# Ten moving tiles of the gate/up matmuls, moved to other SBUF offsets

## The chip, the cores and the metric

The kernel runs on one NeuronCore of a Trainium2 chip. The metric is device microseconds for one execution. The kernel before takes 2365.82 us (median of 2 runs, 2365.75 to 2365.89).

## What is computed

The reference is a two-layer encoder trunk over 1024 tokens of width 1024. Each layer has a combined input projection, three kinds of attention, an output projection, and a SwiGLU feed-forward part. All arrays are float32. The change is in the feed-forward part:

```python
h = rms_norm(x, g_ffn[l]) * (1 + sc_f) + sh_f
gate, up = split_cols(h @ w_gu[l], (FFN_HIDDEN, FFN_HIDDEN))
x = x + gt_f * ((jax.nn.silu(gate) * up) @ w_down[l])
```

`h` is 1024 tokens by 1024 features, `w_gu` is 1024 by 5632, and `FFN_HIDDEN` is 2816.

## The kernel before

Precision. Every float32 operand of a large matmul is split into a high part and a low part (type fp32r), and a product is three matmuls: high weights by high activations, low weights by high activations, high weights by low activations (`mm3`, line 202). The helper `split_to` makes such a pair: ScalarE writes the high part, VectorE or GpSimd the low part.

Gate/up as a fast matrix product. `h` and `w_gu` are cut into 2 by 2 blocks, and a Winograd-like scheme with seven products takes the place of eight (`PRODUCTS`, line 217). The activations are the moving operand, 512 tokens wide. They stand in seven pairs of tiles, made once per layer, each of shape 128 x 4 x 512 with 8192 bytes in a partition: `h21`, `h11`, and `ht2`, `ht1`, `ht4`, `h22`, `ht3`. A letter `h` or `l` at the end of the tile's name is the high or the low part. The helper that allocates them is `h_tiles` (line 2087): `h21` and `h11` come from a pool of their own (`ha`), the other five pairs from the pool `hb`. Both pools are on the right side of SBUF, which is a stack that grows towards lower addresses. The tiles of a pool lie one behind the other, with no space between.

The weights are the stationary operand. `a_parts` (line 233) makes the weight pieces `wpt` (128 x 2 x 4 x 128: high and low part of four blocks of 128 rows) in a ring of eight buffers of 4096 bytes.

The order of work. For each of 22 column groups (`NF`), and for each of the seven products, `product` (line 278) issues four `mm3`, that is twelve matmuls of 128 x 512, into one PSUM bank: `gu_product` (line 2199) then adds, copies or applies the activation. The first seven column groups do products 1 and 2 (`h11`, `h21`) ahead, with weights named `whi` and `wlo`, while `t2_part`, `t3_part` and `t4_part` make the other ten tiles. TensorE works the products in the order h11, h21, ht2, ht1, ht3, h22, ht4. Between the products of the later groups stand now and then two matmuls of another computation (`ps_mod`): their moving operands are `acch` and `accl`, and their weights are the constant tile `onesr`.

Behind gate/up comes the down projection (`ps_d`), whose weights and moving operand are both `wpt` tiles of the same ring. The raw weights of the down projection (`w11`, `w12`, `w21`, `w22`) are loaded by the SP queue into memory that the gate/up tiles held, and so some of these loads wait for TensorE's last reading of such a tile. The SP queue is issued in a fixed order.

Addresses in the built program. A start address within a partition, modulo 256, is called a tile's offset here. In the kernel before, the offset of all fourteen `h` tiles is 96, and so is that of every `wpt`, `whi` and `wlo` tile. `acch` and `accl` lie at 96 too, `onesr` at 128. A slice of an `h` tile starts at a multiple of 2048 bytes and a slice of the weights at a multiple of 512, so that the slices have their tile's offset.

Of the kernel before, what the change touches and what calls it, by code (L numbers as in the profile page):

```python
# [10 lines left out]
F32 = mybir.dt.float32  # L11
F32R = mybir.dt.float32r
# [7 lines left out]
P = 128  # L20
# [3 lines left out]
H = 512  # L24
# [61 lines left out]
def trunk(ctx: ExitStack, tc, A, C, out):  # L86
# [9 lines left out]
    def open_pool(name, bufs=1, side="left", space=None):  # L96
        kw = dict(name=name, bufs=bufs, side=side, reuse_waits="tile")
        if space is not None:
            kw["space"] = space
            if space == PSUM:  # L100
                kw.pop("side")
        cm = tc.tile_pool(**kw)
        p = cm.__enter__()
        return cm, p
# [432 lines left out]
    hl = hp.tile([P, KC, S], F32R, name="hl")  # L537
# [480 lines left out]
    for l in range(2):  # L1018
# [731 lines left out]
        class PairA(Band):  # L1750


            name, by_columns = "sA", True
# [11 lines left out]
        class PairB(Band):  # L1765
            name = "sB"
# [113 lines left out]
        for n in range(-AHEAD - 1, N + 3):  # L1880
# [74 lines left out]
            if n == 60:  # L1955
                t2 = [psS.tile([P, 2, H], F32, name="ps_o", tag="S") for _ in range(2)]
# [127 lines left out]
        ha_cm, hap = open_pool("ha", side="right")  # L2084
        hb = {}

        def h_tiles(pl, names):
            for b in names:
                hb[b] = [pl.tile([P, 4, H], F32R, name=f"h{b}{p}") for p in "hl"]

        h_tiles(hap, ("21", "11"))

        def h_norm(k, half, rows):
# [66 lines left out]

        ff_cm, ffp = open_pool("ffn", side="left")
        hb_cm, hbp = open_pool("hb", side="right")
        h_tiles(hbp, ("t2", "t1", "t4", "22", "t3"))
        turn = [-10]

        def x_tile(n, shape, name):
# [370 lines left out]
        for u in range(NU):  # L2537
# [14 lines left out]
            a, b = ahead.have.pop(0)  # L2552
# [18 lines left out]
            if num == 4:  # L2571
# [6 lines left out]
                else:  # L2578
                    h_cm, hp = open_pool("h", side="right")
                    hh = hp.tile([P, KC, S], F32R, name="hh")  # L2580
                    hl = hp.tile([P, KC, S], F32R, name="hl")
# [121 lines left out]
```

## Time and profile before

| | |
|---|---|
| median of the runs | 2365.82 us |
| span of the profiled execution, first to last instruction | 2365.0 us |
| TensorE busy | 2324.0 us (98%), 11804 matmuls |
| TensorE weight loads busy | 1959.2 us (83%) |
| VectorE / ScalarE / GpSimd busy | 1758.8 / 1185.8 / 778.4 us |
| mean granted TensorE clock | 0.998 |
| gate/up of layer 0, first to last of its matmuls | 552.6 to 981.3 us |
| gate/up of layer 1 | 1709.7 to 2134.9 us |

The profiled execution's own time was not kept beside its span; the span lies 0.8 us below the median of the runs.

How to read it: the matmuls overlap one another, so that a matmul's duration in the profile (389 ns for most with 512 columns) is a latency and not what it costs. What it costs in a stream is the distance from its start to the next matmul's start. The timeline view gives these starts in hundredths of a microsecond; where a row stands for several matmuls (x2), it gives the first one's start.

### The profile page before, as it was taken

Reading aid. Unit: us, or ns where it says so; the run is one execution under the profiler, and the core shown is the slowest. Engines: PE = TensorE matmul, PEld = TensorE weight load, DVE = VectorE, ACT = ScalarE, POOL = GpSimd, SP = SyncE. Lnnn points to the kernel's source line nnn. Section 1 sums busy time; section 2 is a strip of 40 time slices with the busy share of each in tenths; the row PEclk is TensorE's granted clock in tenths of the full one; section 3 lists DMA queues with packets and bytes.
Section 4 is the critical chain, followed back from the end, with each engine's and each line's share of the span. In section 5 each row is a group of like instructions: output and inputs, shape, how many; then the busy total and the mean of one; then the engine's idle time right before and its main releaser. Section 6 shows DMA issues by size and latency. Waiting matters only on the chain. (4 is left out here: it accounts for less than half of the span.)

```text
span 2365.0 us, 33492 instructions
## 1 busy us (share of the span) xinstructions
PE 2324.0 (98%) x11804; PEld 1959.2 (83%) x11804; DVE 1758.8 (74%) x2762; ACT 1185.8 (50%) x2262; POOL 778.4 (33%) x749
## 2 busy tenths in 40 slices
PE   9999999999999999999999999999999999999998
PEld 7888898888788888788888889988878888888886
DVE  7878998869867677595767689897796674538765
ACT  5423889845543333344633268896453434334443
POOL 1530447600444445100145134584005444430001
PEclk9999999999999999999999999999999999999999
DMA  8677416162435544775435851333634443339643
GB/s 281 182 213 232 116 34 185 51 210 94 146 121 166 165 138 141 232 233 181 148 102 139 249 177 28 92 104 104 208 98 139 151 147 103 99 107 305 203 120 112
DMA packets 307450, 358.02 MB, mean 151 GB/s; under 512 B 52029, under 2 KB 223901, under 8 KB 307281
## 3 DMA queue, kind: packets, MB, share of 16 engines
q1 hardware_dynamic: 290784, 346.26, 47.1%
q10 hardware_dynamic: 16128, 9.44, 1.5%
q8 instruction: 93, 1.52, 0.3%
q14 instruction: 77, 0.62, 0.1%
q0 software_dynamic: 368, 0.17, 0.0%
HBM read 270.84 MB, written 88.63 MB: 152 GB/s over the span
## 5 line engine op out<-in xcount | busy, mean ns | idle before, releaser
L49 PE MATMUL ps_d<-wpt 128*128 128x512 f32 x1848 | 423.7, 390 | 1.0 <-ACT wpt L49 0.7
L49 PEld LDWEIGHTS ps_d<-wpt 128*128 128x128 f32 x1848 | 345.7, 188 | 74.3 <-issue 3.0
L49 POOL TENSOR_SCALAR pr<-pr,rs 128x1024 f32<-128x1024 f32 (+2 forms) x248 | 190.7, 785 | 186.8 <-DVE rs L49 166.7
L49 POOL TENSOR_TENSOR sg<-sg,u 128x512 f32<-128x512 f32 x82 | 117.2, 1431 | 348.1 <-ACT sg L49 221.6
L49 ACT CAST wpt<-w 128x512 fp32r<-128x512 f32 x154 | 95.7, 621 | 194.5 <-PE ps_d L49 176.1
L49 PE MATMUL pv<-pt,vs 128*128 128x256 f32 x1088 | 174.0, 296 | 14.3 <-DVE y L49 13.0
L49 DVE TENSOR_TENSOR pt<-T,pt 128x512 fp32r<-128x512 f32 x272 | 177.4, 679 | 7.1 <-ACT pt L49 5.9
L49 ACT CAST pt<-T 128x512 fp32r<-128x512 f32 x272 | 151.7, 586 | 42.9 <-PE T L49 41.4
L49 DVE SCALAR_TENSOR_TENSOR acc<-wmt,condT,acc 128x512 f32<-128x512 f32 (+1 forms) x98 | 115.5, 1186 | 77.1 <-DMA wmt<-in_w_mod_dram 76.3
L49 POOL TENSOR_TENSOR wpt<-ws,wpt 128x512 fp32r<-128x512 f32 x80 | 112.8, 1410 | 181.6 <-ACT wpt L49 136.3
L49 ACT COPY u<-ps_w 128x512 f32<-128x512 f32 x128 | 75.1, 587 | 192.6 <-PE ps_w L49 192.6
L49 DVE TENSOR_TENSOR wpt<-w,wpt 128x512 fp32r<-128x512 f32 x154 | 109.0, 708 | 83.8 <-ACT wpt L49 83.8
L49 PEld LDWEIGHTS pv<-pt,vs 128*128 128x128 f32 x1088 | 141.0, 189 | 26.9 <-DVE y L49 24.9
L49 PE MATMUL T<-identr,pr 128*128 128x128 f32 x1176 | 160.1, 273 | 0.8 <-DVE pt L49 0.4
L49 PEld LDWEIGHTS T<-identr,pr 128*128 128x128 f32 x1176 | 137.8, 140 | 15.8 <-issue 1.3
L49 ACT CAST wpt<-ws 128x512 fp32r<-128x512 f32 x176 | 107.7, 622 | 53.3 <-PE ps_w L49 23.4
L49 DVE TENSOR_TENSOR wpt<-graw,wpt 128x512 fp32r<-128x512 f32 x154 | 110.2, 716 | 17.0 <-ACT wpt L49 17.0
L49 DVE TENSOR_TENSOR wpt<-ws,wpt 128x512 fp32r<-128x512 f32 x96 | 85.2, 896 | 47.6 <-ACT wpt L49 47.4
L49 DVE TENSOR_REDUCE rs<-sC 128x1 f32<-128x1024 f32 x88 | 107.4, 1220 | 12.3 <-PE sC L49 10.9
L49 DVE TENSOR_TENSOR ws<-wr 128x512 f32<-128x512 f32 x88 | 80.3, 913 | 48.5 <-POOL wpt L49 45.1
L49 ACT CAST wpt<-graw 128x512 fp32r<-128x512 f32 x154 | 95.0, 617 | 35.2 <-DMA graw<-gpd 31.0
L49 PE MATMUL ps_w<-h22h,wpt 128*128 128x512 f32 x352 | 108.9, 391 | 2.9 <-ACT u L49 1.9
(310 smaller groups left out, 5936.4 us busy)
## 6 DMA issues: line engine op xcount, KB each, us to landing
wr<-in_w_gu_dram SPq DMA_DIRECT2D x92, 512.0 KB, 4.2
gpd<-sg SPq DMA_DIRECT2D x154, 256.0 KB, 4.4
graw<-gpd SPq DMA_DIRECT2D x76, 512.0 KB, 3.8
w<-in_w_down_dram SPq DMA_DIRECT2D x110, 256.0 KB, 5.2
wmt<-in_w_mod_dram SPq DMA_DIRECT2D x48, 512.0 KB, 5.7
qk<-qkd SPq DMA_DIRECT2D x44, 512.0 KB, 7.3
wst<-in_w_o_dram SPq DMA_DIRECT2D x32, 512.0 KB, 4.3
wmt<-in_w_mod_dram SPq DMA_DIRECT2D x64, 256.0 KB, 4.0
```

Source lines behind the costliest of these rows:

```text
L49: ins = op(*args, **kwargs)
```

## The change

`h_tiles` gets an argument. With it, each tile is followed by a small tile of 8 floats (32 bytes) that nothing writes or reads. The five pairs of the pool `hb` are allocated with it, the two pairs of the pool `ha` without.

```diff
--- before.py
+++ after.py
@@ -2084,9 +2084,13 @@
         ha_cm, hap = open_pool("ha", side="right")
         hb = {}
 
-        def h_tiles(pl, names):
+        def h_tiles(pl, names, apart=0):
             for b in names:
-                hb[b] = [pl.tile([P, 4, H], F32R, name=f"h{b}{p}") for p in "hl"]
+                hb[b] = []
+                for p in "hl":
+                    hb[b].append(pl.tile([P, 4, H], F32R, name=f"h{b}{p}"))
+                    if apart:
+                        pl.tile([P, apart], F32, name=f"pad{b}{p}")
 
         h_tiles(hap, ("21", "11"))
 
@@ -2160,7 +2164,7 @@
 
         ff_cm, ffp = open_pool("ffn", side="left")
         hb_cm, hbp = open_pool("hb", side="right")
-        h_tiles(hbp, ("t2", "t1", "t4", "22", "t3"))
+        h_tiles(hbp, ("t2", "t1", "t4", "22", "t3"), 8)
         turn = [-10]
 
         def x_tile(n, shape, name):
```

The offsets of the ten tiles in the built program, with weights at 96 before and after:

| tile | ht2h | ht2l | ht1h | ht1l | ht4h | ht4l | h22h | h22l | ht3h | ht3l |
|---|---|---|---|---|---|---|---|---|---|---|
| before | 96 | 96 | 96 | 96 | 96 | 96 | 96 | 96 | 96 | 96 |
| after | 32 | 64 | 96 | 128 | 160 | 192 | 224 | 0 | 32 | 64 |

All other tiles keep their addresses. No instruction is added, and on every engine the instructions stand in the order in which they stood. What moves is one wait in each layer. This is the SP queue at the beginning of layer 0's down projection, before the change (`w21`, `w22`, `w12`: raw down weights; `graw`: activations read back; `xb`: the residual; in brackets what the issue waits for, the queue's own semaphores among it):

```order
L49 DMA w12_9686<-in_w_down_dram 128x4x128 [waits DMAHW5_49]
L49 DMA w21_9714<-in_w_down_dram 128x4x128 [waits DMAHW6_49]
L49 DMA w22_9716<-in_w_down_dram 128x4x128 [waits DMAHW7_49]
L49 DMA w12_9718<-in_w_down_dram 128x4x128 [waits DMAHW0_49]
L49 DMA xb_9694<-xd_87 128x512 [waits DMAHW1_49]
L49 DMA graw_9727<-gpd_96 128x1024 [waits DMAHW2_49,DVE_49]
L49 DMA w12_9741<-in_w_down_dram 128x4x128 [waits DMAHW3_49]
L49 DMA xb_9696<-xd_87 128x512 [waits DMAHW4_49]
L49 DMA w21_9765<-in_w_down_dram 128x4x128 [waits DMAHW5_49,PE_49]
```

And the same place after the change:

```order
L49 DMA w12_9696<-in_w_down_dram 128x4x128 [waits DMAHW5_49]
L49 DMA w21_9724<-in_w_down_dram 128x4x128 [waits DMAHW6_49,PE_49]
L49 DMA w22_9726<-in_w_down_dram 128x4x128 [waits DMAHW7_49]
L49 DMA w12_9728<-in_w_down_dram 128x4x128 [waits DMAHW0_49]
L49 DMA xb_9704<-xd_87 128x512 [waits DMAHW1_49]
L49 DMA graw_9737<-gpd_96 128x1024 [waits DMAHW2_49,DVE_49]
L49 DMA w12_9751<-in_w_down_dram 128x4x128 [waits DMAHW3_49]
L49 DMA xb_9706<-xd_87 128x512 [waits DMAHW4_49]
L49 DMA w21_9775<-in_w_down_dram 128x4x128 [waits DMAHW5_49]
```

The wait for TensorE, which belongs to the last reading of `ht3l`, has moved from the third `w21` load to the second, seven issues earlier, because the upper end of the second load's buffer now overlaps the tile that lies 32 bytes lower. The place in layer 1 is the same.

## The prediction

> **What bounds the kernel now.** I read the page's first lines, then a table by stage for the two stretches of gate/up, and then the timeline of TensorE alone.
>
> ```profile
> span 2365.0 us, 33492 instructions
> PE 2324.0 (98%) x11804; PEld 1959.2 (83%) x11804; DVE 1758.8 (74%) x2762; ACT 1185.8 (50%) x2262; POOL 778.4 (33%) x749
> ```
>
> TensorE is busy 98% of the span, so what makes a matmul longer lengthens the kernel unless TensorE waits there for something else. The two gate/up stretches by themselves:
>
> ```profile
> core 0: us, PE busy (x) PEld busy (x) DVE busy (x) ACT busy (x) POOL busy (x), PEclk, DMA share, GB/s
> 552.60:981.30 428.70, 425.35 (x1874) 350.02 (x1873) 311.66 (x400) 175.80 (x308) 168.97 (x117) 1.00 0.45 143
> 1709.70:2134.90 425.20, 422.74 (x1866) 348.68 (x1865) 268.00 (x349) 176.51 (x308) 162.39 (x117) 1.00 0.38 124
> ```
>
> In 428.70 + 425.20 = 853.90 us TensorE is busy 425.35 + 422.74 = 848.09, at the full clock (1.00). It is the bound of this stage; VectorE has 311.66 + 268.00 = 579.66 us of work there. How long TensorE waits for others in the first and in the second stretch, by the view of waits:
>
> ```profile
> PE ps_w L49 <- ACT u L49: 1.8, 2, 0.9
> PE ps_w L49 <- ACT sg L49: 1.5, 3, 0.9
> ```
> ```profile
> PE ps_w L49 <- ACT u L49: 1.8, 2, 1.0
> PE ps_w L49 <- ACT sg L49: 0.7, 2, 0.5
> ```
>
> That is 1.8 + 1.5 + 1.8 + 0.7 = 5.8 us, all of it for ScalarE, which empties TensorE's own banks. At most this much of a slower TensorE could vanish in waits that shrink, and most of it would not, since ScalarE's work there starts when TensorE's ends.
>
> What a matmul costs is read from the starts. TensorE in the middle of gate/up, a product of `ht2` (rows by threes: two matmuls with the high tile, one with the low one):
>
> ```profile
> 2043.76 0.61 PE L49 MATMUL ps_w<-ht2h,wpt 128*128 128x512 f32 x2
> ...
> 2046.26 0.39 PE L49 MATMUL ps_w<-ht2l,wpt 128*128 128x512 f32 x1
> 2046.48 0.61 PE L49 MATMUL ps_w<-ht1h,wpt 128*128 128x512 f32 x2
> ```
>
> From 2043.76 to 2046.48 there are twelve matmuls in 2.72 us: **226.7 ns each**. This is the price with moving tile and weights both at offset 96, and it is what nearly all matmuls of 512 columns pay.
>
> **The change part by part.** It adds no instruction, takes none away and reorders none. It has three effects that could cost time.
>
> The first is the new offset of the moving tiles. How many matmuls read them, from the groups by form (the first and the last of ten rows, five of x352 and five of x176):
>
> ```profile
> L49 PE MATMUL ps_w<-h22h,wpt 128*128 128x512 f32 x352 | 108.9, 391 | 2.9 <-ACT u L49 1.9 <-ACT sg L49 1.0
> ...
> L49 PE MATMUL ps_w<-ht1l,wpt 128*128 128x512 f32 x176 | 68.5, 389 | 0.0
> ```
>
> 5 x 352 + 5 x 176 = **2640 matmuls** in both layers. While one of them streams, the weights of the next are being loaded:
>
> ```profile
> L49 PEld LDWEIGHTS ps_w<-ht2h,wpt 128*128 128x128 f32 x352 | 66.0, 188 | 14.2 <-ACT u L49 0.5
> ```
>
> A load takes 188 ns and lies beside the matmul in front of it, so that two streams of TensorE read SBUF at the same time. Whether they get into each other's way by their addresses can be seen at one place of the trace: the `ps_mod` matmuls, whose moving tiles lie at 96 like all others while their weights, `onesr`, lie at 128. In the attention stage of layer 0:
>
> ```profile
> 217.27 0.39 PE L49 MATMUL ps_ab<-hh,whi 128*128 128x512 f32 x1
> 217.50 0.39 PE L49 MATMUL ps_ab<-hh,wlo 128*128 128x512 f32 x1
> 217.72 0.40 PE L49 MATMUL ps_ab<-hl,whi 128*128 128x512 f32 x1
> 217.96 0.39 PE L49 MATMUL ps_mod<-acch,onesr 128*128 128x512 f32 x1
> 218.19 0.39 PE L49 MATMUL ps_mod<-accl,onesr 128*128 128x512 f32 x1
> 218.42 0.40 PE L49 MATMUL ps_mod<-acch,onesr 128*128 128x512 f32 x1
> 218.65 0.40 PE L49 MATMUL ps_mod<-accl,onesr 128*128 128x512 f32 x1
> 218.89 1.07 PE L49 MATMUL sC<-qk 128*128 128x512 f32 x4
> ```
>
> The first three starts are 0.23 and 0.22 apart, the usual price. The matmul at 217.72 is an ordinary one with its operands at 96, but beside it the first `onesr` is loaded: the next start comes 0.24 later. From 217.72 to 218.89 there are five matmuls in 1.17 us, or 234 ns each, 7 ns above the usual. No wait is shown and the shapes are the usual ones; what is new is an offset that differs by 32 bytes. It isn't shown that the offset is the cause, since `onesr` is also another tile and the PSUM bank changes. It is however the nearest row to the change.
>
> What a differing offset leaves behind is seen at the same pair in gate/up:
>
> ```profile
> 765.62 0.40 PE L49 MATMUL ps_w<-ht4l,wpt 128*128 128x512 f32 x1
> 765.86 0.39 PE L49 MATMUL ps_mod<-acch,onesr 128*128 128x512 f32 x1
> 766.09 0.39 PE L49 MATMUL ps_mod<-accl,onesr 128*128 128x512 f32 x1
> 766.32 0.63 PE L49 MATMUL ps_w<-h11h,wpt 128*128 128x512 f32 x2
> 766.79 0.39 PE L49 MATMUL ps_w<-h11l,wpt 128*128 128x512 f32 x1
> 767.01 0.63 PE L49 MATMUL ps_w<-h11h,wpt 128*128 128x512 f32 x2
> ...
> 767.71 0.62 PE L49 MATMUL ps_w<-h11h,wpt 128*128 128x512 f32 x2
> 768.17 0.39 PE L49 MATMUL ps_w<-h11l,wpt 128*128 128x512 f32 x1
> ```
>
> From 766.32 on the operands are at 96 again. The six matmuls up to 767.71 take 1.39 us, 232 ns each, and only the two from 767.71 to 768.17 are back at 0.46 for two (230 each, rounded to 10 ns in the row). So the stream has a settled pace of 226.7 ns and an unsettled one of about 232, and a disturbance is paid for by several matmuls behind it. In the changed kernel the moving tile's distance to the weights changes between the second and the third matmul of every `mm3`, because the high and the low tile now lie 32 bytes apart modulo 256. I expect that the stream never settles in these products. It makes no difference then that `ht1h` stays at 96, since its neighbour `ht1l` is at 128.
>
> The bounds. From below: no matmul of 512 columns streams faster than the settled pace for long in this trace. The row at 766.79 is followed by a start 0.22 later, 7 ns under it, but slow ones stand on both sides; as a bound for an offset that suits the streams better I take the settled pace less 3 ns, half of that single step, 2640 x 3 ns = 8 us to the good (an estimate). From above: a step of the unsettled stream is at most 0.24, 13 ns over the settled pace: 2640 x 13 = 34 us, if every matmul paid the largest. Both ends come from distances of 0 and 32 bytes, and distances of 64, 96 and 128 stand nowhere in the trace; that is the weak place of this sum. I take the mean of the unsettled stretch in gate/up, 232 - 227 = **5 ns**, since that is the same work on the same engine: 2640 x 5 ns = **13 us**.
>
> The second effect is on the engines that write the ten tiles at their new offsets, 8 casts and 8 subtractions for each pair and two layers. ScalarE's casts of this shape whose source lies at 96, and those where half of the sources (`w12`, `w22`) lie at 160:
>
> ```profile
> L49 ACT CAST wpt<-ws 128x512 fp32r<-128x512 f32 x176 | 107.7, 622 | 53.3 <-PE ps_w L49 23.4 <-issue 22.9 <-DVE ws L49 5.1
> L49 ACT CAST wpt<-w 128x512 fp32r<-128x512 f32 x154 | 95.7, 621 | 194.5 <-PE ps_d L49 176.1 <-DMA w<-in_w_down_dram 12.9 <-issue 3.0
> ```
>
> 622 and 621 ns: nothing, and so I cost it at nothing. If it were 1% of these 80 writes of some 0.6 to 0.7 us, it would be half a microsecond, and it lies beside TensorE's first column groups.
>
> The third is the wait that moved. The second `w21` load stands in the row of four issues at 996.64 of the SP queue (the first row), and it would wait for the last matmul with `ht3l` (the second, from TensorE's timeline):
>
> ```profile
> 996.64 3.18 SPq L49 DMA_DIRECT2D w<-in_w_down_dram  x4
> ```
> ```profile
> 974.18 0.39 PE L49 MATMUL ps_w<-ht3l,wpt 128*128 128x512 f32 x1
> ```
>
> That matmul starts at 974.18, so the load's condition has held for 22 us when the queue comes to it. What stands behind it in the queue (`w22`, `w12`, `xb`, `graw`) waits for nothing new. A TensorE that is 2% later moves both ends alike. Zero.
>
> The sum: 13 us less at most 6 us that waits give back. I give back 1, a share that ScalarE doesn't owe to TensorE: +12 us on the profiled execution's span of 2365.0, 2377. The runs' median lies 0.8 above the span, so **2378 us**, 0.5% slower.
>
> **The rivals.** *The address doesn't matter* (2366). The disturbance at `ps_mod` would be due to the bank or the tile, not to the offset, and the ten tiles would run at 226.7. For it: distances of 256 bytes and more between moving slice and weights occur all the time and show nothing, and the pace in the rows above is the same for all slices. Against it: the slow step comes with the matmul beside which the new weights are loaded, one ahead of the new bank. The Trainium skill speaks for this rival: in "SBUF — State Buffer", section "Who interferes with whom", TensorE has one read port for the moving operand and an independent one for the weights, and "PE and ACT never wait on anyone". By that rule the change is worth nothing and the time stays at 2366; the trace agrees with it in the settled stretches and not at 217.72. The page has no word on offsets.
>
> *A better distance* (2358). Were some distances kinder than zero, the 2640 matmuls would win up to 3 ns each, 8 us. For it speaks only that no other distance is seen in the trace; against it, that all unsettled stretches are slower on average.
>
> *A worse distance* (2392 to 2412). At 64 to 128 bytes the two streams might meet more often than at 32. If each matmul lost 10 to 13 ns, as the largest steps do, it would be 26 to 34 us, 2392 to 2400; up to the bound of 2%, 2413, if a distance lies beyond what the trace has seen.
>
> *The weight load no longer lies beside the matmul* (over 2413, slower than the bound of 2%). If two streams on the same part of SBUF excluded each other, a matmul would cost what it costs where its weights can't be loaded ahead. Such a pair stands behind a change of work:
>
> ```profile
> 562.03 0.48 PE L49 MATMUL ps_w<-h21h,whi 128*128 128x512 f32 x1
> 562.35 0.39 PE L49 MATMUL ps_w<-h21h,wlo 128*128 128x512 f32 x1
> ```
>
> The step from 562.03 to 562.35 is 0.32, 93 ns more than usual; for all 2640 it would be 246 us, 2612. It need not be all: 2% of the kernel is 47 us, or 18 ns per matmul, a fifth of that exposure. It speaks against it that the weights of `onesr`, at another offset, cost 7 ns and not 93.
>
> *The change doesn't do what it says*: the unused tiles could have been laid elsewhere. The addresses in the built program exclude it but for the chip's own way of mapping them, which no row shows; the time would be that of the first rival.
>
> **How the numbers follow.** The forecast, 3 to 7 ns per matmul or 2373 to 2385: 0.52. No effect, the last rival in it: 0.19. A better distance: 0.08. A worse one within 2%: 0.14. Weight loads exposed, over 2%: 0.07. The range from 2358 to 2400 holds the forecast, no effect, most of the better distance and the nearer half of the worse one, some 0.85. Faster by over 2% would need 18 ns off each of the 2640 matmuls, which no row comes near: 0.01, taken from the better distance. Slower by over 2%: 0.07. Within 2%, which is about what a measurement of this kernel can tell from no change: 0.92.
>
> **What would show it.** In the timeline of `ht2`, the twelve matmuls from the first row to the first row of `ht1` should take about 2.78 us in place of 2.72, with steps of 0.22 to 0.24; if they are still 2.72, the first rival holds. By stage, the two gate/up stretches should be 6 us longer each and all others should not move. The products of `h11` and `h21` should be slow only in their first few matmuls. The prediction is wrong if a tile's pace goes by its distance in a way that 32 bytes don't foretell: then the ten tiles would have very different paces, and the ones at 160 to 0 (`ht4`, `h22`) would be the ones to look at. It is also wrong if the time changes outside gate/up, or if SP's queue shows a wait for TensorE near 997 us.

## The result

The changed kernel takes **2379.91 us** (median of 2 runs, 2379.76 to 2380.06) against 2365.82 before: a ratio of 1.0057, 95% interval 1.0041 to 1.0073, or 14.1 us more. The profiled execution's span grew by 13.3 us, from 2365.0 to 2378.3:

```profile
span 2378.3 us, 33492 instructions
PE 2339.2 (98%) x11804; PEld 1959.0 (82%) x11804; DVE 1757.8 (74%) x2762; ACT 1185.5 (50%) x2262; POOL 776.8 (33%) x749
```

TensorE has the same 11804 matmuls and 15.2 us more busy time (2339.2 against 2324.0). The two gate/up stretches by themselves, in the columns of the table by stage that the prediction shows (the stretch, its length, then TensorE's busy time):

```profile
552.90:987.30 434.40, 432.37 (x1874) 350.25 (x1874) 309.99 (x400) 176.18 (x308) 168.41 (x117) 1.00 0.43 141
1716.10:2148.20 432.10, 430.39 (x1866) 348.71 (x1865) 268.48 (x349) 176.39 (x308) 161.55 (x117) 1.00 0.38 122
```

They are 434.40 and 432.10 us long where they were 428.70 and 425.20, so 5.7 and 6.9 us longer, 12.6 of the span's 13.3. What TensorE waits for in them, by the view of waits (first the first stretch, then the second):

```profile
PE ps_w L49 <- ACT u L49: 1.6, 2, 0.9
PE ps_w L49 <- ACT sg L49: 0.4, 1, 0.4
PE ps_w L49 <- ACT u L49: 1.3, 2, 0.7
PE ps_w L49 <- ACT sg L49: 0.4, 1, 0.4
```

That is 1.6 + 0.4 + 1.3 + 0.4 = 3.7 us, where it was 5.8: the slower TensorE gave back 2.1 us in waits that shrank.

The timeline of TensorE in one column group of layer 1 shows the price. The rows with a new tile name are the beginnings of the products:

```profile
2055.57 0.63 PE L49 MATMUL ps_w<-ht2h,wpt 128*128 128x512 f32 x2
...
2058.37 0.61 PE L49 MATMUL ps_w<-ht1h,wpt 128*128 128x512 f32 x2
...
2061.15 0.63 PE L49 MATMUL ps_w<-ht3h,wpt 128*128 128x512 f32 x2
...
2063.95 0.62 PE L49 MATMUL ps_w<-h22h,wpt 128*128 128x512 f32 x2
...
2066.71 0.63 PE L49 MATMUL ps_w<-ht4h,wpt 128*128 128x512 f32 x2
...
2069.51 0.62 PE L49 MATMUL ps_w<-h11h,wpt 128*128 128x512 f32 x2
...
2072.28 0.61 PE L49 MATMUL ps_w<-h21h,wpt 128*128 128x512 f32 x2
...
2075.00 0.63 PE L49 MATMUL ps_w<-ht2h,wpt 128*128 128x512 f32 x2
```

Twelve matmuls of `ht2` take 2058.37 - 2055.57 = 2.80 us, where they took 2.72. The same difference is 2.78 for `ht1`, 2.80 for `ht3`, 2.76 for `h22`, 2.80 for `ht4`. The five together take 2069.51 - 2055.57 = 13.94 us in place of 5 x 2.72 = 13.60, which is 0.34 us for 60 matmuls, or **5.7 ns each**. (The view rounds a start to 10 ns, so that a price per matmul that is read from one product of twelve is good to about 1 ns.) `h11`, whose address did not change, takes 2.77, 0.05 more, in the wake of `ht4`. `h21` behind it is back at 2075.00 - 2072.28 = 2.72.

### The profile page after: what moved, and what is told of

It reads as the page before. It is cut to its first block, busy times and chain, and to the rows that moved or that the text cites. A ratio compares the mean times of both kernels' runs of the same rounds, so it can differ in the third digit from the quotient of the medians.

```text
span 2378.3 us, 33492 instructions
## 1 busy us (share of the span) xinstructions
PE 2339.2 (98%) x11804; PEld 1959.0 (82%) x11804; DVE 1757.8 (74%) x2762; ACT 1185.5 (50%) x2262; POOL 776.8 (33%) x749
## 4 chain that ended last, share of the span: by engine, by line
PE 70%; DVE 4%; issue 3%; ACT 1%; DMA 1%; POOL 1%; SPq 0%; POOLq 0%; ACTq 0%; DVEq 0%
PE ps_w L49 34%; PE ps_d L49 15%; PE ps_o L49 7%; PE ps_ab L49 3%; PE pv L49 3%; PE T L49 2%; PE ps_v L49 2%; PE sC L49 2%; PE ps_c L49 1%; ACT pr L49 1%; PE ps_st L49 0%; DVE xb L49 0%; DMA qk<-qkd 0%; DVE pr L49 0%; DVE pt L49 0%
## 5 line engine op out<-in xcount | busy, mean ns | idle before, releaser
L49 DVE SCALAR_TENSOR_TENSOR acc<-wmt,condT,acc 128x512 f32<-128x512 f32 (+1 forms) x98 | 110.5, 1136 | 76.7 <-DMA wmt<-in_w_mod_dram 75.9
```

The lines of the kernel that those rows point to most:

```text
L49: ins = op(*args, **kwargs)
```

## The experiments

At the start two theories stood against each other that the prediction had not told apart. Theory S (switching): a change of the distance between the moving tile and the weights, both modulo 256, unsettles the stream for some matmuls, and at a constant distance it settles again. Theory D (distance): each distance has its price, whether or not it has just changed. The offset of the weights is 96 in all runs but one. Kernels of one group ran on the same chip and share the runs of the kernel before.

### One distance for all ten tiles

Against the kernel before, one unused tile behind the last moving tile:

```diff
-        h_tiles(hbp, ("t2", "t1", "t4", "22", "t3"))
+        h_tiles(hbp, ("t2", "t1", "t4", "22", "t3"), {"t3l": (56, 32)[l]})
```

Here and below the dictionary gives the floats of unused space behind a tile, and `l` is the layer.

> All ten tiles at one and the same offset: 128 in layer 0 (32 bytes from the weights at 96), 224 in layer 1 (128 bytes). Theory S (switching): only a change of the distance between moving tile and weights unsettles the stream, for some ten matmuls and about 40 ns in all; at a constant distance it settles at 226.7 ns. Then there are two changes in a column group (into ht2, back into h11), about 74 in both layers, 3 us: 2369 us, and ht1, ht3, h22, ht4 at 226.7. Theory D (distance): each matmul pays for its own distance, whether it was changed or not: 2640 matmuls at 232 ns or so, 13 us: 2379 us, with all ten tiles slow and layer 0 unlike layer 1.

Measured: 2380.49 us, ratio 1.0059 (1.0044 to 1.0074). The timeline of a product of `ht1`, first in layer 0 at a distance of 32 bytes, then in layer 1 at 128:

```profile
699.64 0.63 PE L49 MATMUL ps_w<-ht1h,wpt 128*128 128x512 f32 x2
...
702.44 0.63 PE L49 MATMUL ps_w<-ht3h,wpt 128*128 128x512 f32 x2
...
2057.65 0.63 PE L49 MATMUL ps_w<-ht1h,wpt 128*128 128x512 f32 x2
...
2060.45 0.63 PE L49 MATMUL ps_w<-ht3h,wpt 128*128 128x512 f32 x2
```

From 699.64 to 702.44 and from 2057.65 to 2060.45 twelve matmuls take 2.80 us, 233 ns each, although the product before them had the same distance. At a constant distance of 32 or 128 bytes the stream does not come back to 226.7 ns. Theory S falls here, and with it the reason that the prediction gave for the unsettled stream. Theory D had layer 0 unlike layer 1, which did not come: both have 2.80.

### The pairs apart, high and low part together

```diff
-        h_tiles(hbp, ("t2", "t1", "t4", "22", "t3"))
+        h_tiles(
+            hbp, ("t2", "t1", "t4", "22", "t3"),
+            (
+                {"t2l": 8, "t1l": 8, "t4l": 8, "22l": 8, "t3l": 8},
+                {"t2l": 8, "t1l": 48, "t4l": 56, "22l": 56, "t3l": 56},
+            )[l],
+        )
```

> High and low tile of a pair at the same offset, the pairs at different ones: distances to the weights of -32 (ht3), -64 (h22), -96 (ht4), 128 (ht1), 96 (ht2) in layer 0 and 32 (ht3), 64 (h22), 96 (ht4), -96 (ht1), 128 (ht2) in layer 1. Theory S: a change at the beginning of each product, about 250 in both layers, each some 40 ns: 10 us, 2376 us; the last matmuls of each product are at 226.7 in every tile. Theory D: every distance has its own pace through the whole product, 2379 us, and the last matmuls of a product are as slow as the first.

Measured: 2379.32 us, ratio 1.0055 (1.0040 to 1.0070). The time alone hardly tells the two forecasts apart, but the products do. Three products of layer 1, `ht1` at -96 bytes, `h22` at 64 and `ht4` at 96, their beginnings and the last three matmuls of `ht4`:

```profile
2057.93 0.63 PE L49 MATMUL ps_w<-ht1h,wpt 128*128 128x512 f32 x2
...
2060.73 0.63 PE L49 MATMUL ps_w<-ht3h,wpt 128*128 128x512 f32 x2
...
2063.53 0.62 PE L49 MATMUL ps_w<-h22h,wpt 128*128 128x512 f32 x2
...
2066.27 0.63 PE L49 MATMUL ps_w<-ht4h,wpt 128*128 128x512 f32 x2
...
2068.39 0.63 PE L49 MATMUL ps_w<-ht4h,wpt 128*128 128x512 f32 x2
...
2069.09 0.63 PE L49 MATMUL ps_w<-h11h,wpt 128*128 128x512 f32 x2
```

The products take 2.80, 2.74 and 2.82 us, where theory S had 2.72 and some 0.04 for the change. The last three matmuls of `ht4` take 2069.09 - 2068.39 = 0.70 us, 233 ns each: they are not settled, although the distance has been the same for nine matmuls. So distances have prices of their own.

### Only the low parts apart

```diff
-        h_tiles(hbp, ("t2", "t1", "t4", "22", "t3"))
+        h_tiles(
+            hbp, ("t2", "t1", "t4", "22", "t3"),
+            {b + p: n for b in ("t2", "t1", "t4", "22", "t3") for p, n in (("h", 8), ("l", 56))},
+        )
```

> The five high tiles stay at 96, the five low tiles go to 128: distances 0, 0, 32 in every group of three matmuls. Theory S: the distance changes twice in every group of three, the stream never settles, and all 2640 matmuls run at about 232: 2379 us, as with the whole change. Theory D: only the 880 matmuls with a low tile pay, 5 to 7 ns each: 4 to 6 us, 2371 us, with the high tiles at 226.7.

Measured: 2378.03 us, ratio 1.0048 (1.0033 to 1.0063). A product of `ht2` in layer 1, where the high tile is at distance 0 and the low one at 32:

```profile
2054.64 0.62 PE L49 MATMUL ps_w<-ht2h,wpt 128*128 128x512 f32 x2
2055.09 0.40 PE L49 MATMUL ps_w<-ht2l,wpt 128*128 128x512 f32 x1
2055.33 0.63 PE L49 MATMUL ps_w<-ht2h,wpt 128*128 128x512 f32 x2
2055.79 0.40 PE L49 MATMUL ps_w<-ht2l,wpt 128*128 128x512 f32 x1
2056.03 0.63 PE L49 MATMUL ps_w<-ht2h,wpt 128*128 128x512 f32 x2
2056.49 0.39 PE L49 MATMUL ps_w<-ht2l,wpt 128*128 128x512 f32 x1
2056.72 0.63 PE L49 MATMUL ps_w<-ht2h,wpt 128*128 128x512 f32 x2
2057.19 0.39 PE L49 MATMUL ps_w<-ht2l,wpt 128*128 128x512 f32 x1
2057.42 0.61 PE L49 MATMUL ps_w<-ht1h,wpt 128*128 128x512 f32 x2
```

The product takes 2.78 us, 232 ns each. Behind the first low matmul (at 2055.09, 0.24) the matmuls with the high tile are slow too: the first pair takes 0.45, the next three 0.46, 0.46 and 0.47, so that these six take 1.39 us where six at 226.7 would take 1.36. The four low ones take 0.94. Theory D in its plain form falls as well, since it had only the low tiles pay and 2371 us. The time is the one that theory S had here, 2379, although its reason has fallen above: each of the two theories had one of these runs right and the other wrong. What is left holds both findings: **of the distances tried only 0 has the pace of 226.7 ns, and a matmul that disturbs the stream is paid for by those behind it, at distance 0 too**, until that pace is back.

### All at 128

The kernel before with everything but the two constants `identr` and `onesr` moved by 32 bytes: weights and moving tiles both at 128.

```diff
     onesr = cp.tile([P, P], F32R, name="onesr")
...
+    pad(cp, 8)
     epst = cp.tile([P, 1], F32, name="epst")
...
-    pad(ctx.enter_context(tc.tile_pool(name="rpad", bufs=1, side="right")), 32)
+    pad(ctx.enter_context(tc.tile_pool(name="rpad", bufs=1, side="right")), 24)
```

> The kernel before with all tiles but the two constants shifted by 32 bytes: moving tiles and weights both at 128 instead of 96, so that no distance among them changes, and the ps_mod weights (onesr, at 128) now lie at distance 0. Theories S and D (only the distance counts): 2365 to 2366 us, and the five steps around ps_mod are at 226.7 instead of 234 (40 such matmuls, under 1 us in all). Theory A (the offset itself counts, 96 is a good place and 128 a bad one): some 8000 matmuls of 512 columns at 5 ns more, 2405 us.

Measured: 2365.38 us, ratio 0.9996 (0.9987 to 1.0006). It is the distance that counts and not the offset. The place of the prediction's main row, where `onesr` (still at 128) now has distance 0:

```profile
218.20 0.39 PE L49 MATMUL ps_ab<-hl,whi 128*128 128x512 f32 x1
218.43 0.39 PE L49 MATMUL ps_mod<-acch,onesr 128*128 128x512 f32 x1
218.65 0.39 PE L49 MATMUL ps_mod<-accl,onesr 128*128 128x512 f32 x1
218.88 0.39 PE L49 MATMUL ps_mod<-acch,onesr 128*128 128x512 f32 x1
219.11 0.39 PE L49 MATMUL ps_mod<-accl,onesr 128*128 128x512 f32 x1
219.33 0.84 PE L49 MATMUL sC<-qk 128*128 128x512 f32 x3
```

From 218.20 to 219.33 five matmuls take 1.13 us, 226 ns each, where five took 1.17. Tiles, banks and order are those of before, and only the distance is gone: what the prediction read at this place as the nearest row to the change, without having shown it, was the distance. There are only 40 such matmuls, so that the gain does not show in the time.

The step in front of a mismatched pair goes the same way. In gate/up, the last matmul before `ps_mod`:

```profile
766.63 0.39 PE L49 MATMUL ps_w<-ht4l,wpt 128*128 128x512 f32 x1
766.85 0.39 PE L49 MATMUL ps_mod<-acch,onesr 128*128 128x512 f32 x1
```

Its step is 0.22 us here and was 0.24 before (765.62 to 765.86, in the prediction's rows), although its own weights lie at distance 0 in both kernels. What differs is the next matmul, whose weights are loaded beside this one. Whether that load is what costs the time, or the next matmul's own start, can't be told apart here, since both have their moving tiles at the same offset.

### The same movement, all distances 0

Each pair of tiles made one tile with 256 unused bytes behind it:

```diff
-                hb[b] = [pl.tile([P, 4, H], F32R, name=f"h{b}{p}") for p in "hl"]
+                t = pl.tile([P, 8 * H + room], F32R, name=f"h{b}")
+                t = t[:, at : at + 8 * H].rearrange("p (z k n) -> p z k n", z=2, n=H)
+                hb[b] = [t[:, 0], t[:, 1]]
...
-        h_tiles(hbp, ("t2", "t1", "t4", "22", "t3"))
+        h_tiles(hbp, ("t2", "t1", "t4", "22", "t3"), 64, 0)
```

> Each pair of high and low tile is made one tile with 256 unused bytes behind it: the addresses move by up to 1280 bytes, as the allocation of the loads behind them does, but all distances modulo 256 stay 0. Theory D (the distance modulo 256 counts): all ten tiles at 226.7 ns, 2365 to 2366 us. Theory P (the space between tiles, the loads that overlap other tiles or their moved wait cost the time): 2375 to 2380 us as with the change.

Measured: 2366.36 us, ratio 1.0003 (0.9994 to 1.0013). The tiles' names are cut to `ht` and `h` here, so that `ht2`, `ht1` and `ht3` stand in one row of 36 matmuls:

```profile
2064.58 8.32 PE L49 MATMUL ps_w<-ht,wpt 128*128 128x512 f32 x36
2072.74 2.88 PE L49 MATMUL ps_w<-h,wpt 128*128 128x512 f32 x12
```

2072.74 - 2064.58 = 8.16 us for 36, 226.7 ns each. Unused space and moved addresses cost nothing when the distances modulo 256 stay 0.

### Smaller distances, and 64 both ways

The same kernel with `at` 4 and 1 floats (16 and 4 bytes) in layer 0 and layer 1, and with 2 and 60 floats (8 and -16 bytes); and the kernel with one distance for all, with 48 and 16 floats behind the last tile (64 and -64 bytes). One run each:

```diff
-        h_tiles(hbp, ("t2", "t1", "t4", "22", "t3"), 64, 0)
+        h_tiles(hbp, ("t2", "t1", "t4", "22", "t3"), 64, (4, 1)[l])
...
+        h_tiles(hbp, ("t2", "t1", "t4", "22", "t3"), 64, (2, 60)[l])
...
-        h_tiles(hbp, ("t2", "t1", "t4", "22", "t3"), {"t3l": (56, 32)[l]})
+        h_tiles(hbp, ("t2", "t1", "t4", "22", "t3"), {"t3l": (48, 16)[l]})
```

> As the run with pairs 256 bytes apart, but the tiles begin 16 bytes (layer 0) and 4 bytes (layer 1) behind the weights' offset. Theory X (any distance that is not 0 keeps the stream from settling): both layers at 229 to 234 ns, gate/up 6 to 7 us longer in each, 2378 us. Theory U (distances count in units of 32 bytes or so): both layers at 226.7, 2366 us. In between: layer 0 slow and layer 1 at 226.7, 2372 us, which would put the unit between 4 and 16 bytes.

> As the run with 16 and 4 bytes, with distances of 8 bytes (layer 0) and -16 bytes (layer 1). Theory X: both layers at 229 to 234 ns, 2378 us. Theory U: both at 226.7, 2366 us. If only the size of the distance counts, layer 1 has the pace that 16 bytes have.

> All ten tiles at one distance, 64 in layer 0 and -64 in layer 1. In the run with the pairs apart, h22 at 64 was at 228.8 behind a tile at 32, and at -64 at 233.7 behind a tile at -32. If the distance sets the pace, layer 0 has 229 in all tiles (gate/up 3 us longer) and layer 1 has 233 to 234 (9 us longer in its 1320 matmuls): 2377 us. If the tile in front sets it, both layers have the same pace in all tiles.

Measured: 2383.67, 2380.09 and 2375.61 us, beside 2365.86 before (13 runs, 2362.51 to 2371.06). Products of twelve matmuls, two rows for each layer. Distances 16 and 4 bytes (`h22`):

```profile
704.89 2.94 PE L49 MATMUL ps_w<-h,wpt 128*128 128x512 f32 x12
707.67 2.94 PE L49 MATMUL ps_w<-ht,wpt 128*128 128x512 f32 x12
...
2066.02 3.00 PE L49 MATMUL ps_w<-h,wpt 128*128 128x512 f32 x12
2068.86 3.00 PE L49 MATMUL ps_w<-ht,wpt 128*128 128x512 f32 x12
```

2.78 us at 16 bytes and 2.84 at 4. This kernel differs from the one with all distances 0 only in where the tiles begin within their space. Distances 8 and -16:

```profile
704.92 2.96 PE L49 MATMUL ps_w<-h,wpt 128*128 128x512 f32 x12
707.72 2.96 PE L49 MATMUL ps_w<-ht,wpt 128*128 128x512 f32 x12
...
2063.81 2.96 PE L49 MATMUL ps_w<-h,wpt 128*128 128x512 f32 x12
2066.61 2.96 PE L49 MATMUL ps_w<-ht,wpt 128*128 128x512 f32 x12
```

2.80 at both. Distances 64 and -64 (`ht1`):

```profile
698.65 0.62 PE L49 MATMUL ps_w<-ht1h,wpt 128*128 128x512 f32 x2
...
701.39 0.62 PE L49 MATMUL ps_w<-ht3h,wpt 128*128 128x512 f32 x2
...
2053.97 0.63 PE L49 MATMUL ps_w<-ht1h,wpt 128*128 128x512 f32 x2
...
2056.77 0.63 PE L49 MATMUL ps_w<-ht3h,wpt 128*128 128x512 f32 x2
```

2.74 and 2.80, as was forecast for the case that the distance sets the pace and not the tile in front. Theory X came and theory U falls: there is no unit of 32 bytes within which a distance is free, and 4 bytes are the dearest of all, above the 229 to 234 ns that theory X had. That only the size of the distance counts is out by 64 and -64. The prices, per matmul of 512 columns, each from the start of one product to the next, divided by twelve:

| distance, bytes | 0 | 4 | 8 | 16 | 32 | 64 | 96 | 128 | -96 | -64 | -16 |
|---|---|---|---|---|---|---|---|---|---|---|---|
| product, us | 2.72 | 2.84 | 2.80 | 2.78 | 2.80 | 2.74 | 2.82 | 2.80 | 2.80 | 2.80 | 2.80 |
| ns per matmul | 226.7 | 237 | 233 | 232 | 233 | 228 | 235 | 233 | 233 | 233 | 233 |

The values at 96 and -96 are from the pairs apart, where the neighbours' distances are others.

## Why the prediction was right

- **The bound.** TensorE set the pace of gate/up, and what its matmuls lost went into the time: 12.6 of 13.3 us lie in the two stretches, as forecast (6 us each; 5.7 and 6.9).
- **The size of the first term.** It was put at 5 ns for 2640 matmuls, 13 us. Measured are 5.7 ns in a column group, which would be 15 us for 2640, and 0.05 us for each product of `h11` that follows `ht4`. In the two stretches TensorE's busy time grew by a little less, 7.02 + 7.65 = 14.7 us with `h11` in it; some products had been above 226.7 before the change too, as the one behind `ps_mod` that the prediction shows. The price came from that unsettled stretch; a product of `ht2` was forecast at 2.78 us and took 2.80, the ten tiles' products 2.76 to 2.80. The prediction counts six unsettled matmuls in the stretch. In the trace's nanoseconds the two that it calls back still take 232 and 231, and only then 227 follows, so that they are eight.
- **The give-back.** 1 us was taken off for waits that shrink; 2.1 us went. The two differences have opposite signs: 14.7 - 2.1 = 12.6 us in the stretches against a forecast of 12. The other 0.7 us of the span lie outside them (0.3 before the first, 0.4 between the two), where the forecast had nothing and no run shows what they are.
- **The nearest row.** That the slow steps at `ps_mod` come from the offset was taken as likely and called not shown. The kernel with all at 128 showed it: the steps there went from 234 to 226 ns. The rival that the address doesn't matter is out: with addresses changed and no instruction, twelve matmuls take 2.80 us in place of 2.72. The rule of the Trainium skill ("SBUF — State Buffer", "Who interferes with whom") that TensorE never waits on anyone is out by the same two numbers, as far as it is read to cover TensorE's own two streams.
- **The reason for the unsettled stream.** This step was wrong. The prediction had the stream unsettled because high and low tile differ by 32 bytes, so that the distance changes within each `mm3`. With one constant distance it is just as slow (2.80 us): a constant distance other than 0 suffices. For the one constant distance this reason had given 2369 us, and 2380.49 was measured. That the number came out all the same is in part luck. The 5 ns were read from matmuls at distance 0 behind a disturbance, and it happens that the distances of the change cost about as much by themselves; at 64 bytes for all ten tiles they would cost 2 ns, at 4 bytes 10. That a pace goes by its distance was the prediction's own sign of being wrong. The sign did not show in the change, whose products lie within 2.76 and 2.80 us, but the table above has such paces, 2.72 to 2.84 us.
- **`ht1h` at 96 makes no difference.** Nearly right: `ht1` took 2.78 against 2.80 for `ht2`, so that a high tile at distance 0 beside a low one at 32 is a little cheaper, as in the run with only the low parts apart (2.78).
- **A better distance.** None of the ten other distances in the table is faster than 0; the nearest is 64, with 2.74.
- **A worse distance, and the weight load exposed.** The dearest measured is 4 bytes with 10 ns; no distance came near the 93 ns of a load that isn't hidden.
- **What can be told from no change.** The prediction put this at about 2%. The interval of the measured ratio, 1.0041 to 1.0073, is much narrower.
- **The wait that moved.** It cost nothing that shows. The loads concerned stand in the first row below, of the SP queue's timeline (four issues, the second load of `w21` among them). The last matmul with `ht3l`, in the second row, starts 24 us earlier, and the view of the queue's waits (985 to 1015 us) has no wait for a gate/up matmul. Its only wait for TensorE is the third row, 0.6 us for a matmul of the down projection between 1000 and 1003 us, ahead of these loads. It was not there before the change, so that the prediction's sign of being wrong, a wait of SP for TensorE near 997 us, came by its letter. It is another matmul's wait, though, and layer 1, where there is such a wait of 0.7 us, takes 230.1 us from the end of gate/up to the end of the span in both kernels:

```profile
1003.91 2.56 SPq L49 DMA_DIRECT2D w<-in_w_down_dram  x4
```
```profile
980.18 0.39 PE L49 MATMUL ps_w<-ht3l,wpt 128*128 128x512 f32 x1
```
```profile
SPq L49 <- PE ps_d L49: 0.6, 1, 0.6
```

## What to carry to other kernels

Where TensorE is the bound and streams fp32r matmuls of 512 columns, give the moving tiles and the weights the same start address modulo 256: here a mismatch cost 2 to 10 ns of 227 per matmul, with no instruction added. Look for it in the timeline, in the distance from one start to the next; the mean durations move by 2 to 12 ns (`h22h` from 391 to 393, `ht4l` from 389 to 401) and no wait is shown. And when one mismatched matmul stands in a stream, count those behind it too: eight behind the pair at 766.32, but hardly more than one behind the four `ps_mod` matmuls of the attention stage at 176.19, where the nine from 177.34 to 179.38 take 2.04 us, 226.7 ns each.

## What the runs showed that was not expected

- A stream at a distance other than 0 does not come to 226.7 ns, however long the distance stays the same: 2.80 us for a product at 32 and at 128 bytes, against 2.72 at 0. It can be steady all the same: at -64 every group of three in the product shown takes 0.70 us, where 0.68 is the pace at 0.
- The price does not follow the size of the distance: 10 ns at 4 bytes, 5 at 16, 6 to 7 at 8, 32 and 128, 2 at 64, and -64 (2.80 us) is unlike 64 (2.74). Nor is a mixture the mean of its parts. With the distances 0, 0 and 32 a product takes 2.78 us, where two thirds of 2.72 and one third of 2.80 make 2.75. `h22` in the changed kernel, at 128, 128 and -96, takes 2.76, where products at either distance alone take 2.80.
- Why it is so stays open. That the two reads of TensorE, of the moving tile and of the next weights, meet in the memory is only argued from the place where the first slow step stands, beside the load of the mismatched weights. That this step, too, goes with the distance is shown (0.24 against 0.22 us). No run took the weight load away, and whether the distance to the next weights or to the matmul's own counts was not tried, as all weights in gate/up share one offset.
